# A two-layer hybrid mixer on one core: three steps of the recurrent stage start later in the program, their readers of transferred data are held in program order, and two half modulation vectors move to TensorE

## The chip, the core and the metric

The program runs on one NeuronCore of one Trainium2 chip. The metric is device time in microseconds (us) of one execution. The engines are TensorE (PE, with its weight loads PEld), VectorE (DVE), ScalarE (ACT), GpSimd (POOL) and SyncE (SP), which here issues all the transfers (DMAs). Each engine takes its instructions in one fixed order; an instruction that waits holds everything behind it on that engine.

## The reference, cut to what matters

Two layers over 1024 latent tokens and 256 context tokens of width 1024:

```python
for l in range(DEPTH):
    sh1, sc1, gt1, sh2, sc2, gt2 = split(silu(c) @ w_mod[l] + b_mod[l], 6)   # modulation; the same for c_ctx
    ux = _modulate(h, norm1_g[l], sh1, sc1) @ w_in[l]          # 17 column blocks of 128
    uc = ...                                                   # the same weights on the context
    y_rwkv = _rwkv_mixer(ux, uc, ...)                          # both directions, context state first
    h = h + gt1 * (concat([y_rwkv, pool(ux), fourier(ux), conv(ux)]) @ w_out[l])
    h = h + gt2 * _swiglu(_modulate(h, norm2_g[l], sh2, sc2), ffn_w_in[l], ffn_w_out[l])
    # the context stream hc likewise, in the first layer only
return _rmsnorm(h, final_norm_g)

# _rwkv_mixer, per head and token, in each direction:
S_t = S_{t-1} diag(w_t) + (S_{t-1} (-kk_t)) (a_t * kk_t)^T + v_t k_t^T ;  y_t = S_t r_t
```

## The kernel before

Activations stand with channels on the 128 partitions. A float32 matmul is kept exact enough by splitting each operand in a high and a low half (`split`, L317: ACT copies the high half, DVE or POOL takes the difference) and three products.

**A layer.** `rwkv1` makes the projections that the recurrence needs, while a side generator (convolution and pooling) and, in the first layer, the generators of six half modulation vectors (`s.mods`: j = 2, 3, 4 in two halves) are stepped between them. A half vector is made either by `mod_sum` (L240: for each of 8 slices of the weights, the slice times a scalar, added up, for two right-hand sides: on DVE where half is 1, on ACT and POOL where it is 0) or by `mod_pe` (8 matmuls of 512 columns with a 2-column stationary operand, a copy, 4 small matmuls). `MODPE` names those made by `mod_pe`.

**The recurrent stages** (`rwkv2`). The recurrence is done in blocks of 128 tokens, two directions at a time: 2 stages over the context and 8 over the latent, in each layer; 20 in all. Stage j goes through these steps, in different rounds `it` of the loop, each round having 14 gaps (`GAPS`):

- `prep`: decays and scaled keys (a scan on DVE, L917, and products on DVE and POOL).
- `inner`: products of keys (PE), masked by DVE into the tiles W (L982, four per stage); eight small DMAs write them to DRAM (Ad, L986), two of 256 KB bring them back spread over the partitions (As, L992). Then the solve: a triangular inverse by 8 rounds of small DVE instructions (L1020 to L1041; a small part on POOL, behind a memset of the tile, L1018). Its result goes by one DMA to DRAM (Td, L1045) and by four back into TT (L1051).
- `front_b`: the joining of the two half blocks of the inverse. DVE transposes TT (L1091), PE and ACT do two small steps (L1103, L1120); W gets a copy of the keys by DMA (L1109).
- `chain`: the recurrence itself, a row of PE steps and ACT copies, with products on POOL (L1147).
- `finish`: the read-out; DMAs bring back the other direction's part (L1196), DVE adds it (L1207).

Between the steps `W.step()` moves every live generator on by one `yield`, and `W.fill` hands PE a fixed amount of other work: first the remaining projections and the Fourier mixing, later the output projection of the blocks that are ready (`outp`, L1638). A generator that yields `None` gives up the filling of that gap.

The code sets an order only loosely: the framework rearranges the instructions of each engine by a priority list against its own estimate of when inputs are ready. `s.ahead(SPRI)` puts the solve's instructions ahead. `keep_in_program_order` ties an instruction behind the one that was written before it on the same engine.

Of the kernel before, what the change touches and what calls it, by code (L numbers as in the profile page):

```python
# [11 lines left out]
ALU = mybir.AluOpType  # L12
# [4 lines left out]
D = 1024  # L17
# [11 lines left out]
GAPS = 14  # L29
MLAG = 3  # L30
# [8 lines left out]
OLAG = 4  # L39
SIDEP = 2  # L40
MODP = 2
MODPE = ((3, 0),)
# [48 lines left out]
class _Kernel:  # L91
# [61 lines left out]
    @contextmanager  # L153
    def ahead(s, by):

        s.tc.cur_priority -= by
        yield
        s.tc.cur_priority += by

# [157 lines left out]
    def split(s, src, hi, lo, eng=None):  # L317
        s.nc.scalar.copy(hi, src)  # L318
        (eng or s.lo_eng).tensor_tensor(lo, src, hi.bitcast(F32), ALU.subtract)  # L319

# [472 lines left out]
    def rwkv2(s, R, fill):  # L793

        hss = [("c", i) for i in range(2)] + [("x", i) for i in range(8)]
        N = len(hss)
# [4 lines left out]
        for it in range(-3, N):  # L801
# [9 lines left out]
            for g in range(GAPS):  # L811
                if g == 0:
                    if 0 <= it + 1 < N:
                        if it == -1:
                            s.states(R, F[0])
                            for h in range(2):
                                s.nc.gpsimd.memset(F[0].VS[h][64 * h:64 * h + 64, :], 0.0)
                        tb_ = W.start(s.front_b(R, F[it + 1]))
                    if it >= 1 and F[it - 1].rd:
                        W.start(s.finish(R, F[it - 1]))  # L820
                if g == GAPS // 2 and 0 <= it + 2 < N:
                    F[it + 2].v = s.slices(R, "v", F[it + 2], "v")
# [14 lines left out]
            for t in (tb_ if 0 <= it + 1 < N else None, tx.get(it + 2), tp if it + 3 < N else None):  # L837
                W.drain(t)
# [125 lines left out]
    def inner(s, R, F):  # L964
# [30 lines left out]
        for d in range(2):  # L995
# [8 lines left out]
            yield  # L1004
        s.lab(f"rsolve.{F.seg}{F.i}")
# [8 lines left out]
        for a in range(2):  # L1014
# [3 lines left out]
            nc.gpsimd.memset(at(x, 16 * a, [33, 16]), 1.0)  # L1018
            with s.ahead(SPRI):
                e.tensor_tensor(t(0, [1, 2]), D(34, [33, 2]), D(1, [33, 2]), ALU.mult)  # L1020
# [37 lines left out]
    def front_b(s, R, F):  # L1058
# [4 lines left out]
        for p in range(2):  # L1063
            nc.scalar.copy(vr[:, p * 128:(p + 1) * 128], s.nat(F.v, p, 1))
# [26 lines left out]
        nc.vector.transpose(T1.rearrange("q (u i) -> q u i", i=32), TTv[:, :, 0:32])  # L1091
# [89 lines left out]
    def finish(s, R, F):  # L1181
# [20 lines left out]
        yield  # L1202
        yield
        lab()
        for t_, w_ in ((y, w[0]), (ks, w[1])):
            hv = lambda a: a.rearrange("q (d n) -> q d n", d=2)
            nc.vector.tensor_tensor(hv(t_), hv(t_), hv(w_)[:, ::-1, :], ALU.add)  # L1207
# [429 lines left out]
    def outp(s, l, tb, hi_, ho, ymix):  # L1637
# [5 lines left out]
        acts = []  # L1643
        for k in ks:
# [7 lines left out]
            s.split(y, *a)  # L1652
            acts.append(a)
            yield 0.1
# [222 lines left out]
```

## Time and profile before

| | |
|---|---|
| median of 3 runs | 3368.19 us (3366.14 to 3374.23) |
| the profiled execution | 3355.82 us; its span 3354.0 us |
| busy share of the span | PE 88%, PEld 71%, DVE 64%, POOL 42%, ACT 38% |
| mean granted TensorE clock | 0.912 of full speed |
| recurrent stages, first layer | about 462 to 924 us of the span |
| recurrent stages, second layer | about 2182 to 2610 us |

Times in the views are from the start of the span. A view of waits says which engine sat idle, at which line, until what. In the table by stretch the columns are busy time of each engine with the number of instructions, the granted clock (1.00 is 2.4 GHz), the busy share of the 16 DMA engines and GB/s.

### The profile page before, as it was taken

What the parts mean: (1) busy time and instruction counts of PE and PEld (TensorE: products, weight loads), DVE (VectorE), ACT (ScalarE), POOL (GpSimd) and SP (SyncE); (2) the same over time, 40 slices, a digit from 0 to 9 for tenths busy, and PEclk for the clock granted to TensorE, in tenths of its full rate; (3) what the DMA queues carried; (4) which work ended last, traced back from release to release, by engine and by line L of the source; (5) the groups of instructions that cost most, each with busy time, mean ns of one, the idle gap of its engine ahead of it and who ended that gap; (6) DMA issues with size and microseconds to landing.
All of it is one profiled execution on the core that took longest, in us unless ns stands there. A gap on an engine that the chain in (4) does not pass through costs nothing.

```text
span 3354.0 us, 52362 instructions
## 1 busy us (share of the span) xinstructions
PE 2962.7 (88%) x18872; PEld 2391.2 (71%) x18872; DVE 2136.8 (64%) x3524; ACT 1261.7 (38%) x2575; POOL 1395.4 (42%) x1490
## 2 busy tenths in 40 slices
PE   6978898777989999999999978878776699999998
PEld 3757766665778888887888766645554478888887
DVE  6799766666566888644535597666575655555435
ACT  4555435344463322223212455333433433333312
POOL 2465324554268544444310154245541265454600
PEclk8979887788899999999999988878877799999999
DMA  7433345555464444336412222345553322224512
GB/s 265 148 99 105 102 117 143 148 152 156 142 215 153 143 134 151 112 106 225 141 29 90 75 69 95 106 130 142 163 143 83 129 76 82 88 76 134 171 40 77
DMA packets 375818, 415.48 MB, mean 124 GB/s; under 512 B 115587, under 2 KB 214916, under 8 KB 375558
## 3 DMA queue, kind: packets, MB, share of 16 engines
q1 hardware_dynamic: 375558, 412.13, 39.5%
q8 instruction: 149, 2.44, 0.3%
q14 instruction: 111, 0.91, 0.1%
HBM read 306.49 MB, written 100.27 MB: 121 GB/s over the span
## 4 chain that ended last, share of the span: by engine, by line
PE 58%; DVE 21%; DMA 11%; issue 4%; SPq 2%; ACT 2%; POOL 1%; DVEq 0%; POOLq 0%; ACTq 0%
PE pc L151 17%; PE ps L151 17%; PE pb L151 14%; PE pf L151 10%; DVE c L525 4%; DMA t<-Ad 3%; DMA Td<-t 2%; DVE t L1039 2%; DVE t L1032 1%; DVE t L255 1%; DVE t L947 1%; DVE g L1040 1%; DVE t L1041 1%; DVE f L319 1%; DMA Ad<-t 1%
## 5 line engine op out<-in xcount | busy, mean ns | idle before, releaser
L151 PE MATMUL pc<-t,f 128*128 128x512 f32 (+1 forms) x3108 | 744.8, 389 | 31.4 <-ACT t L420 18.7
L151 PEld LDWEIGHTS pc<-t,f 128*128 128x128 f32 x3108 | 575.3, 193 | 160.3 <-ACT t L420 22.9
L151 PE MATMUL ps<-t,f 128*128 128x512 f32 (+1 forms) x2094 | 517.7, 392 | 21.3 <-ACT t L318 7.6
L151 PE MATMUL pb<-t,f 128*128 128x512 f32 (+1 forms) x2094 | 467.5, 368 | 7.8 <-ACT t L1457 3.6
L151 PEld LDWEIGHTS ps<-t,f 128*128 128x128 f32 x2094 | 390.6, 190 | 102.2 <-ACT t L318 8.1
L151 PEld LDWEIGHTS pb<-t,f 128*128 128x128 f32 x2094 | 368.7, 189 | 77.7 <-ACT t L1457 4.4
L1504 ACT CAST f<-c 128x512 fp32r<-128x512 f32 x316 | 195.8, 621 | 529.3 <-PE ps L151 127.7
L1506 POOL TENSOR_TENSOR f<-c,f 128x512 fp32r<-128x512 f32 x135 | 185.8, 1377 | 429.3 <-ACT f L1504 424.2
L151 PE MATMUL pf<-t,f 128*128 128x512 f32 (+2 forms) x1500 | 311.1, 361 | 20.9 <-DMA f<-eo 10.0
L151 PEld LDWEIGHTS pf<-t,f 128*128 128x128 f32 (+1 forms) x1500 | 247.5, 197 | 66.5 <-issue 10.4
L318 ACT CAST f<-m 128x512 fp32r<-128x512 f32 (+1 forms) x236 | 135.5, 577 | 413.4 <-PE pb L151 218.6
L1506 DVE TENSOR_TENSOR f<-c,f 128x512 fp32r<-128x512 f32 x181 | 161.8, 894 | 139.5 <-ACT f L1504 134.5
L523 POOL TENSOR_TENSOR c<-c,cp 128x352 f32<-128x352 f32 (+2 forms) x168 | 185.4, 1104 | 151.5 <-ACT c L516 91.8
L151 PE MATMUL pf<-c,f 128*128 128x512 f32 (+1 forms) x704 | 212.0, 431 | 8.5 <-DVE t L1669 7.2
L319 POOL TENSOR_TENSOR t<-c,t 128x512 fp32r<-128x512 f32 (+1 forms) x110 | 138.1, 1294 | 163.0 <-PE ps L151 100.2
L151 PE MATMUL ps<-t,t 64*128 64x128 f32 (+2 forms) x1032 | 156.1, 342 | 54.9 <-DVE t L947 32.4
L151 PEld LDWEIGHTS ps<-t,t 64*128 64x128 f32 (+1 forms) x1032 | 129.9, 230 | 82.8 <-issue 26.3
L525 DVE SCALAR_TENSOR_TENSOR c<-c,dv,c 128x352 f32<-128x352 f32 (+2 forms) x238 | 186.9, 819 | 1.0
L255 DVE SCALAR_TENSOR_TENSOR cp<-m,sc,cp 128x512 f32<-128x512 f32 x140 | 138.5, 1010 | 51.9 <-DMA m<-in_wmod 51.1
L151 PE MATMUL pc<-t,t 128*64 128x64 f32 (+3 forms) x2484 | 137.8, 246 | 33.8 <-ACT t L1165 19.7
L151 PEld LDWEIGHTS pc<-t,t 128*64 128x64 f32 (+2 forms) x2484 | 111.9, 151 | 76.8 <-issue 24.4
L151 PEld LDWEIGHTS pf<-c,f 128*128 128x128 f32 x704 | 137.4, 222 | 39.8 <-DVE t L1669 7.8
(256 smaller groups left out, 4760.6 us busy)
## 6 DMA issues: line engine op xcount, KB each, us to landing
c<-in_ffin SPq DMA_DIRECT2D x176, 256.0 KB
m<-in_wmod SPq DMA_DIRECT2D x116, 256.0 KB
t<-rw SPq DMA_DIRECT2D x232, 128.0 KB
hid<-t SPq DMA_DIRECT2D x88, 256.0 KB
c<-hid SPq DMA_DIRECT2D x88, 256.0 KB
m<-in_ffout SPq DMA_DIRECT2D x80, 256.0 KB
t<-in_wmod SPq DMA_DIRECT2D x76, 256.0 KB
m<-in_win SPq DMA_DIRECT2D x64, 256.0 KB
```

The lines of the kernel that those rows point to most:

```text
L151: s.nc.tensor.matmul(o, l, r, start=start, stop=stop)
L255: nc.vector.scalar_tensor_tensor(acc[t], w, sc, acc[t], ALU.mult, ALU.add)
L318: s.nc.scalar.copy(hi, src)
L319: (eng or s.lo_eng).tensor_tensor(lo, src, hi.bitcast(F32), ALU.subtract)
L523: nc.gpsimd.tensor_tensor(g, g, t_, ALU.add)
L525: nc.vector.scalar_tensor_tensor(a, w[:, j:j + m], tap(j), a, ALU.mult, ALU.add)
L947: nc.vector.tensor_tensor(BKv[rows, :, :, 1 - h, :], cv(kd)[rows], cv(iP)[rows], ALU.mult)
L1032: nc.vector.tensor_tensor(tv, at(x, o, [0, m], [1, 4], [32, 4]), at(T_, r0, [32, m], [0, 4], [1, 4]), ALU.mult)
L1039: nc.vector.tensor_tensor(tv, at(x, o + 4, [0, m], [1, n], [32, 4]), at(T_, r0, [32, m], [0, n], [1, 4]), ALU.mult)
L1040: nc.vector.tensor_reduce(uv, tv, mybir.AxisListType.X, ALU.add)
L1504: nc.scalar.copy(hi, x)
L1506: (nc.gpsimd if s.nw % 7 in LOP else nc.vector).tensor_tensor(lo, x, hi.bitcast(F32), ALU.subtract)
```

## The change

```diff
-MLAG = 3
+MLAG = 6
+SLAG = 2
+FLAG = 4
-MODPE = ((3, 0),)
+MODPE = ((2, 1), (3, 0), (4, 1))
+    def pin(s, i):
+        return s.tc.keep_in_program_order(i)
...
     def split(s, src, hi, lo, eng=None):
-        s.nc.scalar.copy(hi, src)
+        r = s.nc.scalar.copy(hi, src)
         (eng or s.lo_eng).tensor_tensor(lo, src, hi.bitcast(F32), ALU.subtract)
+        return r
...
+                if g == GAPS // 2:
+                    W.drain(tx.get(it + 1))
...
-            for t in (tb_ if 0 <= it + 1 < N else None, tx.get(it + 2), tp if it + 3 < N else None):
+            for t in (tb_ if 0 <= it + 1 < N else None, tp if it + 3 < N else None):
                 W.drain(t)
...
+        for _ in range(SLAG):
+            yield
         s.lab(f"rsolve.{F.seg}{F.i}")
...
-            nc.gpsimd.memset(at(x, 16 * a, [33, 16]), 1.0)
+            s.pin(nc.gpsimd.memset(at(x, 16 * a, [33, 16]), 1.0))
             with s.ahead(SPRI):
-                e.tensor_tensor(t(0, [1, 2]), D(34, [33, 2]), D(1, [33, 2]), ALU.mult)
+                s.pin(e.tensor_tensor(t(0, [1, 2]), D(34, [33, 2]), D(1, [33, 2]), ALU.mult))
...
-            nc.scalar.copy(vr[:, p * 128:(p + 1) * 128], s.nat(F.v, p, 1))
+            s.pin(nc.scalar.copy(vr[:, p * 128:(p + 1) * 128], s.nat(F.v, p, 1)))
...
-        nc.vector.transpose(T1.rearrange("q (u i) -> q u i", i=32), TTv[:, :, 0:32])
+        s.pin(nc.vector.transpose(T1.rearrange("q (u i) -> q u i", i=32), TTv[:, :, 0:32]))
...
-        yield
-        yield
+        for _ in range(FLAG):
+            yield
         lab()
...
-            nc.vector.tensor_tensor(hv(t_), hv(t_), hv(w_)[:, ::-1, :], ALU.add)
+            s.pin(nc.vector.tensor_tensor(hv(t_), hv(t_), hv(w_)[:, ::-1, :], ALU.add))
...
-            s.split(y, *a)
+            late.append((y, a))
             acts.append(a)
+        for _ in range(OLAG):
+            yield None
+        for y, a in late:
+            s.pin(s.split(y, *a))
             yield 0.1
```

The joining waits six yields instead of three, the solve two more, the read-out four instead of two; a solve may now run on into the next round and is completed at its middle gap. In `outp` the loads of a block are all issued, four gaps without filling follow, then the splits.

On DVE, around the start of the sixth solve of the first layer (its working tile is g_1091 before, g_1086 and g_1147 of two solves after), the order before was: the last reduction of the solve before, two of the four masks of this stage, the transpose of the TT that has just been sent off, two additions of the output projection, the new solve.

```order
L1033 TENSOR_REDUCE t2_744_3437<-t2_744_3437 128x8x4
L982 TENSOR_TENSOR t2_892_4342<-ps_1068_5700,cv_73 128x512
L982 TENSOR_TENSOR t2_894_4344<-ps_1069_5701,cv_73 128x512
L1091 STREAM_TRANSPOSE t2_925_4533<-t2_881_4303 128x256
L1669 SCALAR_TENSOR_TENSOR t2_1056_5600<-pf_1057_5602,mod0_78,t2_1056_5600 128x256
L1669 SCALAR_TENSOR_TENSOR t2_1076_5736<-pf_1077_5738,mod0_78,t2_1076_5736 128x256
L1020 TENSOR_TENSOR g_1091_5863<-t2_721_3310 128x4x2
```

On DVE after the change, at the start of the seventh solve of that layer, the last mask (L991) stands before the end of the solve before:

```order
L991 TENSOR_TENSOR t2_703_3190<-ps_1121_6147,cv_73 128x512
L1052 TENSOR_TENSOR t2_855_4076<-t2_855_4076,g_1086_5810 128x6x8
L1043 TENSOR_TENSOR t2_855_4076<-t2_722_3289,t2_855_4076 128x112
L1044 TENSOR_REDUCE t2_855_4076<-t2_855_4076 128x7x4
L1050 TENSOR_TENSOR t2_855_4076<-t2_722_3289,t2_855_4076 128x112
L1051 TENSOR_REDUCE g_1086_5810<-t2_855_4076 128x28
L1052 TENSOR_TENSOR t2_855_4076<-t2_855_4076,g_1086_5810 128x7x4
L1043 TENSOR_TENSOR t2_855_4076<-t2_722_3289,t2_855_4076 128x128
L1044 TENSOR_REDUCE t2_855_4076<-t2_855_4076 128x8x4
L1684 SCALAR_TENSOR_TENSOR t2_1131_6222<-pf_1132_6224,mod0_78,t2_1131_6222 128x256
L1684 SCALAR_TENSOR_TENSOR t2_1141_6282<-pf_1142_6284,mod0_78,t2_1141_6282 128x256
L1031 TENSOR_TENSOR g_1147_6347<-t2_721_3288 128x4x2
```

The transpose has moved out of this place. On DVE after the change it stands inside the seventh solve, 15 instructions behind its start:

```order
L1044 TENSOR_REDUCE t2_749_3454<-t2_749_3454 128x2x4
L1050 TENSOR_TENSOR t2_749_3454<-t2_721_3288,t2_749_3454 128x192
L1051 TENSOR_REDUCE g_1147_6347<-t2_749_3454 128x48
L1052 TENSOR_TENSOR t2_749_3454<-t2_749_3454,g_1147_6347 128x2x24
L1102 STREAM_TRANSPOSE t2_865_4144<-t2_980_4871 128x256
L926 SCALAR_TENSOR_TENSOR t2_682_3063<-t2_592_2604,t2_663_2960 128x512
```

Over the 20 stages the rows between the last mask and the solve's first instruction on DVE were 70 and are 123; the rows between the end of a solve and the transpose of its result were 2 to 7 in 16 stages and are 16 to 36 in 18. On SP, at the same place before, the four reads of TT (L1051) stood between the writes of Ad and its reads (L992):

```order
L1045 DMA Td1059_5634<-t2_744_3437 4x256x32
L986 DMA Ad1064_5668<-t2_892_4342 32x4x32 x2
L1661 DMA t2_1088_5828<-hd223_865 128x256
L1051 DMA t2_881_4303<-Td1059_5634 32x8x32 x4
L867 DMA t2_746_3469<-rw255_897 128x2x128
L1661 DMA t2_1098_5915<-hd224_866 128x256
L986 DMA Ad1064_5668<-t2_894_4344 32x4x32 x2
L1670 DMA ho213_855<-t2_1056_5600 128x256
L296 DMA m2_1108_6034<-in_wout 128x512
L992 DMA t2_721_3310<-Ad1064_5668 128x1x512
L992 DMA t2_722_3311<-Ad1064_5668 128x1x512
```

On SP after the change, for the same stage:

```order
L995 DMA Ad1055_5593<-t2_889_4308 32x4x32 x2
L995 DMA Ad1055_5593<-t2_891_4310 32x4x32 x2
L995 DMA Ad1055_5593<-t2_890_4309 32x4x32 x2
L995 DMA Ad1055_5593<-t2_892_4311 32x4x32 x2
L1056 DMA Td1062_5664<-t2_749_3454 4x256x32
L1676 DMA t2_1072_5724<-hd221_863 128x256
L1001 DMA t2_721_3288<-Ad1055_5593 128x1x512
L1001 DMA t2_722_3289<-Ad1055_5593 128x1x512
L1062 DMA t2_904_4380<-Td1062_5664 32x8x32 x4
```

The reads of TT have gone behind the reads of Ad here. Over the 20 stages they stood ahead of them in 10 and do so in 8.

## Rows read from the trace of the kernel before

**Rows 1.** The page: busy time by engine, and the chain that ended last.
```profile
PE 2962.7 (88%) x18872; PEld 2391.2 (71%) x18872; DVE 2136.8 (64%) x3524; ACT 1261.7 (38%) x2575; POOL 1395.4 (42%) x1490
...
PE 58%; DVE 21%; DMA 11%; issue 4%; SPq 2%; ACT 2%; POOL 1%; DVEq 0%; POOLq 0%; ACTq 0%
```
**Rows 2.** Stretches: first layer's modulations, the filling after, both layers' recurrent stages.
```profile
160.00:360.00 200.00, 157.45 (x784) 124.52 (x784) 197.03 (x294) 110.87 (x214) 115.26 (x113) 0.84 0.31 99
360.00:462.00 102.00, 98.51 (x589) 80.51 (x587) 64.64 (x152) 36.91 (x85) 26.05 (x55) 0.98 0.44 127
462.00:924.00 462.00, 376.78 (x3825) 289.35 (x3826) 295.58 (x641) 193.78 (x498) 218.81 (x342) 0.81 0.51 144
2182.00:2610.00 428.00, 315.23 (x3319) 231.47 (x3317) 261.19 (x586) 161.29 (x427) 180.60 (x307) 0.78 0.46 129
```
**Rows 3.** Six solve-to-solve stretches of the first layer (588 to 870), summed.
```profile
sum 282.00, PE 221.21 PEld 176.74 DVE 183.21 ACT 114.76 POOL 150.27; mean PE 36.87 PEld 29.46 DVE 30.54 ACT 19.13 POOL 25.04
```
**Rows 4.** Line L992 (reads of Ad): who waited for it, us and times.
```profile
  POOL t L1018: 206.6, 20
  DVE g L1020: 143.6, 20
```
**Rows 5.** Line L1091 (transpose of TT): what it waited for, then who waited for it.
```profile
  DMA t<-Td: 68.0, 15
...
  PE pb L151: 23.8, 3
```
**Rows 6.** DVE, from the end of one solve to the next (start, length, engine, line).
```profile
620.24 0.29 DVE L1033 TENSOR_REDUCE t<-t 128x32 f32<-128x128 f32 x1
...
623.49 0.69 DVE L982 TENSOR_TENSOR t<-ps,cv 128x512 f32<-128x512 f32 x1 [2.37 <-PE ps L151]
628.29 0.45 DVE L1091 STREAM_TRANSPOSE t<-t 128x256 f32<-128x256 f32 x1 [4.11 <-DMA t<-Td]
628.66 0.83 DVE L1669 SCALAR_TENSOR_TENSOR t<-pf,mod,t 128x256 f32<-128x256 f32 x2
636.63 0.17 DVE L1020 TENSOR_TENSOR g<-t 128x8 f32<-128x8 f32 x1 [7.14 <-DMA t<-Ad]
```
**Rows 7.** SP in the same time.
```profile
625.43 1.79 SPq L1051 DMA_DIRECT2D t<-Td  x4
...
628.55 0.86 SPq L986 DMA_DIRECT2D Ad<-t  x2
...
630.88 1.15 SPq L992 DMA_DIRECT2D t<-Ad  x2
```
**Rows 8.** DVE, a solve with no read of TT between.
```profile
2440.90 1.28 DVE L982 TENSOR_TENSOR t<-ps,cv 128x512 f32<-128x512 f32 x2
2450.80 0.17 DVE L1020 TENSOR_TENSOR g<-t 128x8 f32<-128x8 f32 x1 [5.77 <-DMA t<-Ad]
```
**Rows 9.** DVE, transposes outside such a gap, first and last of five.
```profile
676.14 0.45 DVE L1091 STREAM_TRANSPOSE t<-t 128x256 f32<-128x256 f32 x1 [6.64 <-DMA t<-Td]
...
2578.96 0.45 DVE L1091 STREAM_TRANSPOSE t<-t 128x256 f32<-128x256 f32 x1 [4.12 <-DMA t<-Td]
```
**Rows 10.** The chain of waits from 500 us: two reads of Ad.
```profile
504.57 6.26 DMA t<-Ad
...
547.97 9.23 DMA t<-Ad
```
**Rows 11.** DVE, 100 to 310 us: busy time of line L255 (count).
```profile
100.00:310.00 210.00, 40.25 (x42) 0.88 0.39 124
```
**Rows 12.** PE, one matmul of a half vector.
```profile
155.70 1.02 PE L151 MATMUL pf<-t,sc 128*2 128x512 f32 x2
```
**Rows 13.** Line L1646 (loads of the output projection): who waited.
```profile
  ACT c L318: 38.8, 11
```
**Rows 14.** Line L1669 (the output projection's addition): all of them.
```profile
L1669 DVE SCALAR_TENSOR_TENSOR t<-pf,mod,t x40: 443/740/753, 628.7 to 2495.1; 128x512 f32<-128x512 f32 x32, 128x256 f32<-128x256 f32 x8
```

More of the change, by code (lines that the diff above doesn't have):

```diff
@@ L1642, in outp @@
         s.lab("outp")
-        acts = []
+        acts, late = [], []
         for k in ks:
```

## Prediction

> **What bounds the kernel now.** I read the page first: PE is busy for 88% of the span, and the chain that ended last is 58% PE, 21% DVE and 11% DMA [rows 1]. So most of the span is bound by PE and this change does not touch it; what can be won lies where PE stands still. The table by stretch shows where: between 160 and 360 us DVE is busy for 197.0 of 200 us and PE for 157.5, so DVE sets the pace; the 102 us behind it are PE's again (98.5). In the recurrent stages PE is busy for 376.8 of 462 us in the first layer and 315.2 of 428 us in the second, at a mean granted clock of 0.81 and 0.78, and DVE for about two thirds: neither is full, so waits set the pace there [rows 2]. The reader is to see that about 198 us of PE's time stand idle in the two stretches of stages, and 42 us in the first one.
>
> The waits come next. DVE's first instruction of a solve waited 143.6 us in 20 solves for the reads of Ad, POOL's memset 206.6 us [rows 4]; the transpose of TT waited 68.0 us in 15 of 20 [rows 5]. One stage shows how they stand: the solve ends at 620.53, the last mask at 624.18, the transpose waits 4.11 us for Td until 628.29, the next solve 7.14 us for Ad until 636.63 [rows 6]. DVE thus did 2.7 us of work in 16.1 us. SP explains part of it: the four reads of TT stand ahead of the last writes of Ad, and these are issued only at 628.55, 4.4 us after the last mask; the reads of Ad follow at 630.88 [rows 7]. Where no read of TT stands between, 8.6 us passed from the last mask to the solve [rows 8], against 12.4 us here.
>
> **The stages, part by part.** The sum is made against the profiled execution, 3355.8 us, which is 12.4 us below the median of 3368.2; I add these at the end.
>
> *Delays, pins and the moved draining* go together, since what they do is one new order. Three things follow on DVE.
> - Order on SP: in ten stages the reads of TT stood ahead of the reads of Ad, now in eight. Two stages at 12.4 - 8.6 = 3.8 us: 8 us.
> - The transpose: it now stands 15 or more rows inside a solve, after its TT has long landed, so its 68.0 us go. But most of that wait lay between the last mask and the solve, where DVE would have waited for Ad anyway, as in rows 6. Only five waits lay elsewhere, 2.6 to 6.6 us each, 23.4 us in all [rows 9]. I count 23.
> - The solve: between the last mask and its start 123 rows stand now, 70 before. A row takes 295.58/641 to 261.19/586 us, 0.45 us [rows 2], so 53 rows cover 24 us of the wait for Ad.
>
> Together DVE is held 55 us less. The bounds: at most 143.6 + 68.0 = 212 us, if every one of these waits went; below nothing if the wait only moves to another engine (rivals). The 55 us are not all the kernel's. A stage lasts 47 us (282/6) and DVE works in 30.5 and PE in 36.9 of them [rows 3]: a stage of 44 us leaves PE 7 us of slack, so PE does not close the gap, but some stages will wait for PE, ACT or POOL next. I take three quarters, 41 us, since the transpose and the solve's first instruction sit on the engine whose order decides when the next stage's products and masks come.
>
> How far the wait for Ad can fall by order: the read of 256 KB alone took 6.26 and 9.23 us in the chain [rows 10]. Either it queues behind other transfers, then an earlier place shortens it too; or it is slow in itself. The Trainium skill, "DMA: Bandwidth & Descriptors", "Rules for kernel authors", says that an outermost dimension of fewer than 16, such as a broadcast of c copies, keeps a transfer on at most c of the 16 engines; this read broadcasts 4 copies outermost. By that rule the read stays near its 6 us whatever the order, and the sum stays as above; by the other reading up to 3 us a solve, 60 us in 20, would be added to it. No row here counts the engines of one transfer. I add nothing.
>
> *The read-out's two more yields and its pin, the pinned copy of v:* DVE and ACT no longer stop for transfers that come late; the waits are single and short, and ACT and DVE have slack there. Nothing, from -10 to +10 us.
>
> *The output projection's loads.* ACT waited 38.8 us in 11 of its splits for them [rows 13]; ACT is busy for less than half of the stages [rows 2], so little of that reached PE. Against it stand four more gaps without filling for each of five blocks. `FILL` gives 0.9 us of PE's time to a gap: 3.6 us a block, three blocks in the first layer, 10.8 us of matmuls that move behind the stages, where PE is full. In the second layer the filling ended at 2495 [rows 14], with stages until 2610, so it costs nothing. Between -10 and +11 us; I take 0.
>
> **The modulation vectors.** Two `mod_sum` on DVE go: 2 x 8 slices x 2 instructions, 32, at 40.25/42 = 0.96 us [rows 11]: 31 us less for DVE, in the stretch that DVE bounds. Added on PE are 16 matmuls at 1.02 us [rows 12], 16 us; the small ones at the end replace others as small. Their weight loads (DMAs) are the same. In this stretch DVE goes from 197 to 166 us and PE from 157 to 173: it can shorten by 200 - 173 = 27 us at most, and if PE stays late for other reasons the 16 us may come on top. Bounds -27 to +16; since after it PE is the bound and DVE's convolution work is spread over the steps of the generators, I take a little under half of the gain, 12 us.
>
> **Sum:** 3355.8 - 41 - 12 = 3303 us in the profiled execution, 3315 us beside the median.
>
> **Rivals.**
> *The waits move and do not go (0.16).* Four solves of 20 still have no row between the last mask and their start, and the read of Ad takes as long as ever; what DVE no longer waits at the transpose it waits at the solve, and the 41 us shrink to nothing. For it: most of the transpose's wait did lie under Ad's. Against it: the five waits elsewhere, and 53 rows. Then only the modulations are left, in full or in part: 3356 to 3368 us; I put 3358.
> *The gap closes wholly (0.10).* The 16.1 us from one solve's end to the next, with 2.7 us of work, shrink to the 8.6 us that the read path needs at least, counted from a mask that now comes before the solve's end: 7.5 us in 17 stages, 128 us; three quarters is 96, with the modulations 108, and 3260 us. For it: the first layer's later stages all have their reads of Ad first. Against it: the second layer's order gained little.
> *PE stalls at the joining (0.14), the slower side.* The transpose comes a third of a stage later, and the joining and the chain's next step stand behind it on PE. It already stopped PE three times, 23.8 us, 7.9 us each [rows 5]. In the new order the transpose is behind the solve's own wait for Ad and some 15 rows (7 us). If PE reaches the joining before that in nine stages of 20, it stalls 9 x 7.9 = 71 us, 47 more than now, and the chain behind it as well; DVE's gain is then used up by the masks that wait for PE. With 10 us for the modulations: 3368 + 47 - 10 = 3405 us. It decides from about five such stages on (5 x 7.9 = 40 us, the gain that I count in the stages). Against it: between the joining and the chain's use of it stand matmuls of the filling.
>
> **How the numbers follow.** The forecast has 0.60; within it, with the transpose and solve terms anywhere from a third to all of what DVE loses less, and the modulations from 0 to 27 us, its own range is 3265 to 3350. The range given for 8 in 10 adds the whole closing of the gap below and the moved waits and the mildest stalls above: 3250 to 3372. A measurement of this kernel can tell 0.3%, 10 us, from no change. Faster by more than that: 0.60 + 0.10 + 0.06 (the moved waits with the modulations' gain in full) = 0.76; within: 0.10; slower: 0.14.
>
> **What would show it.** Right, step by step: the waits of the transpose for Td are below 10 us in all; those of the solve's first DVE instruction fall from 143.6 to about 110 us; line L255's successor has 32 instructions fewer before 310 us and DVE is no longer full from 160 to 360 us, while that stretch ends 10 to 25 us earlier; a solve follows the last in about 44 us instead of 47. Wrong: the same 47 us with waits of DVE for PE at the masks, or of PE for the transpose above 40 us; a wait for Ad that grows by what the transpose lost; PE's busy time in the stages unchanged with its idle time at other lines.

## The result and the profile after

Sixteen runs of each kernel on the same chips: before 3360.7 us (median, 3351.3 to 3376.1), after 3343.3 us (3335.2 to 3351.5). The ratio is **0.9941, 95% interval 0.9930 to 0.9953**: 20 us faster. The forecast was 53 us. The sign was right and the time lies in the range, but the range reached from no gain at all to the whole closing of the gap, so that says little for the mechanism. The size was not right, and the question is where 33 us stayed.

The profile's page of the changed kernel: busy times by engine, and the chain that ended last (compare [rows 1]). The profiled execution took 3351.4 us, 8 us over its median.

```profile
PE 3000.7 (90%) x18888; PEld 2410.5 (72%) x18888; DVE 2109.8 (63%) x3498; ACT 1257.5 (38%) x2575; POOL 1385.8 (41%) x1484
...
PE 55%; DVE 14%; DMA 9%; issue 3%; SPq 1%; ACT 1%; POOL 1%; DVEq 0%; POOLq 0%; ACTq 0%
```

These shares can't be set beside those before: they add up to 84% here and to 99% there, because this chain could be followed back only to 514 us of the span. Its first rows are:

```profile
514.17 0.14 DVE t L1052
514.39 0.31 DVE t L1043
```

From 550 us to the end, where both chains are whole, DVE's share is 17.5% before and 16.4% after, and DMA's 10.3% and 10.2%: the chain hardly changed. The stretches, columns as in [rows 2]; the two last end at the last read-out of each layer, which comes 12 us earlier in the first (910 for 922) and 16 us earlier in the second (2594 for 2610, though that layer's first solve starts 11 us later):

```profile
160.00:360.00 200.00, 176.01 (x857) 135.91 (x856) 176.07 (x267) 115.85 (x222) 115.52 (x118) 0.87 0.27 90
360.00:462.00 102.00, 99.20 (x593) 81.95 (x592) 61.49 (x149) 37.40 (x87) 25.19 (x50) 0.98 0.41 121
462.00:910.00 448.00, 362.50 (x3662) 276.71 (x3660) 272.98 (x626) 177.62 (x467) 199.21 (x326) 0.79 0.50 141
2190.00:2594.00 404.00, 324.82 (x3307) 241.04 (x3305) 260.27 (x587) 158.64 (x425) 179.74 (x307) 0.79 0.49 137
```

DVE is no longer full from 160 to 360 us (176 us busy, 197 before). TensorE stands idle in the first layer's stages for 85 us as before (448.0 - 362.5, before 462.0 - 376.8); in the second layer's for 79 us in place of 113. Who waited for the reads of Ad, us and times (L1001, which was L992: [rows 4]); then what the transpose waited for, and who for it (L1102, which was L1091: [rows 5]):

```profile
  POOL t L1029: 173.3, 33
  DVE g L1031: 125.5, 17
```

```profile
  DMA t<-Td: 8.3, 5
...
  PE pb L153: 5.6, 5
```

So the waits went the way that was forecast: the transpose's for Td from 68.0 to 8.3 us, DVE's for Ad from 143.6 to 125.5 (about 110 was forecast), and PE waits less for the transpose than before (5.6 us for 23.8). By these waits the change does most of what it should; by the time it does a good third.

**One table for all that follows.** From each kernel's profile, by DVE's first instruction of a solve and the end of the last instruction of a read-out: A, start to first solve; B+C, from there to the second layer's first solve (B: to the first layer's last read-out); D, from there to the last read-out; E, the rest. "Pace" is the mean time between solves from the fifth to the tenth of a layer. These are single profiles. Where two kernels hold the same instructions up to the end of D (the changed one and the one with hidden halves on DVE), B differed by 8.5 us and D by 5.6, so a difference of that size in the table can be chance.

| kernel | A | B | B+C | D | E | pace, 1st / 2nd layer | ratio to before (95%) |
|---|---|---|---|---|---|---|---|
| before | 389.8 | 533.0 | 1725.8 | 495.4 | 743.1 | 47.4 / 44.8 | 1 |
| stages alone | 390.3 | 534.0 | 1732.6 | 485.4 | 751.1 | 48.0 / 44.6 | 0.9988 (0.9975 to 1.0000) |
| projection alone | 389.7 | 525.1 | 1743.6 | 487.7 | 742.8 | 46.2 / 43.6 | 1.0002 (0.9989 to 1.0016) |
| modulations alone | 386.4 | 526.4 | 1724.7 | 490.2 | 741.9 | 45.7 / 46.0 | 0.9957 (0.9941 to 0.9974) |
| all but projection | 387.7 | 533.5 | 1731.5 | 484.7 | 744.2 | 47.9 / 44.2 | 0.9967 (0.9952 to 0.9981) |
| all but modulations | 391.3 | 518.6 | 1737.4 | 474.7 | 745.0 | 44.5 / 43.0 | 0.9962 (0.9950 to 0.9974) |
| after | 389.2 | 521.3 | 1737.5 | 468.0 | 754.9 | 45.4 / 42.6 | 0.9941 (0.9930 to 0.9953) |
| before, fast reads | 388.4 | 505.2 | 1698.2 | 456.1 | 743.6 | 42.2 / 41.4 | 0.9799 (0.9785 to 0.9813) |
| after, fast reads | 384.3 | 485.9 | 1700.8 | 456.2 | 741.1 | 40.6 / 39.5 | 0.9795 (0.9773 to 0.9818) |
| best | 387.2 | 504.0 | 1697.6 | 439.1 | 742.1 | 45.2 / 38.3 | 0.9720 (0.9692 to 0.9747) |

### The profile page after: what moved, and what is told of

Same layout as the page of the kernel before. It is cut to its first block, busy times and chain, and to the rows that moved or that the text cites. A ratio compares the mean times of both kernels' runs of the same rounds, so it can differ in the third digit from the quotient of the medians.

```text
span 3349.6 us, 52386 instructions
## 1 busy us (share of the span) xinstructions
PE 3000.7 (90%) x18888; PEld 2410.5 (72%) x18888; DVE 2109.8 (63%) x3498; ACT 1257.5 (38%) x2575; POOL 1385.8 (41%) x1484
## 4 chain that ended last, share of the span: by engine, by line
PE 55%; DVE 14%; DMA 9%; issue 3%; SPq 1%; ACT 1%; POOL 1%; DVEq 0%; POOLq 0%; ACTq 0%
PE pc L153 17%; PE ps L153 17%; PE pb L153 14%; PE pf L153 8%; DMA t<-Ad 3%; DVE c L532 2%; DMA Td<-t 1%; DVE t L1050 1%; DVE t L947 1%; DVE t L1043 1%; DVE f L325 1%; DVE t L956 1%; DVE t L1469 1%; DMA t<-ho 1%; DVE t L1493 1%
## 5 line engine op out<-in xcount | busy, mean ns | idle before, releaser
L153 PE MATMUL pc<-t,f 128*128 128x512 f32 (+1 forms) x3108 | 754.4, 392 | 41.3 <-ACT t L427 16.0
L153 PE MATMUL pf<-c,f 128*128 128x512 f32 (+1 forms) x704 | 200.5, 416 | 30.0 <-DVE t L1684 20.3
L153 PEld LDWEIGHTS pc<-t,t 128*64 128x64 f32 (+2 forms) x2484 | 124.6, 161 | 71.8 <-issue 28.6
L153 PE MATMUL pc<-t,t 128*64 128x64 f32 (+3 forms) x2484 | 156.2, 258 | 20.9 <-DMA t<-t 11.8
```

Source lines behind the costliest of these rows:

```text
L153: s.nc.tensor.matmul(o, l, r, start=start, stop=stop)
```

## The parts, one by one

The first four runs leave parts out or make one alone. out_undo is the changed kernel with this edit, mod_undo with the next one, stage_only with both; out_only is the kernel before with the first edit the other way round.

```diff
-            late.append((y, a))
+            s.split(y, *a)
             acts.append(a)
-        for _ in range(OLAG):
-            yield None
-        for y, a in late:
-            s.pin(s.split(y, *a))
             yield 0.1
```

```diff
-MODPE = ((2, 1), (3, 0), (4, 1))
+MODPE = ((3, 0),)
```

> Only the delays, the pinned readers of the stages and the moved draining; output projection and modulation vectors as before. Theory (the stages gain about 40 us, the output projection's new gaps give some 20 us back, the modulations do nothing): ratio to the kernel before 0.988 to 0.990, some 37 us less; the matmuls of the filling between 600 and 922 us number about 548 again, against 480 in the changed kernel. Rival A (the 20 us lost behind the first layer's stages come from the later read-out of the context, which holds the filling back): ratio 0.994, 480 matmuls. Rival B (the two modulation vectors on TensorE cost what is lost): 0.989 as well, but the next run then parts it from the theory.

> The changed kernel with the two half modulation vectors on DVE again. Theory: ratio to before 0.993 to 0.995, the same as the changed kernel within 3 us, with DVE busy about 197 us again between 160 and 360 us. Rival B (they cost 16 us of TensorE that nothing pays back): 0.989. Forecast's own term (they win 12 us): 0.998.

> The changed kernel with the output projection's splits directly behind their loads and without the four gaps that give up their filling. Theory: 0.988 to 0.990, 15 to 20 us faster than the changed kernel, with about 548 matmuls of the filling between 600 and 922 us and the waits of ACT for the loads back at some 39 us. Rival A (later read-out of the context): 0.994, as the changed kernel.

> The kernel before with the output projection's change alone. Theory: 10 to 20 us slower than before, ratio 1.003 to 1.006, since the matmuls that the new gaps give up run behind the first layer's stages, where TensorE is full. Rival A: no change, 0.999 to 1.001. The forecast's term was 0 with bounds of -10 and +11 us.

Measured: 0.9988, 0.9962, 0.9967, 1.0002. My theory failed in all four. I had read section B in the two profiles (12 us shorter) as the stages' gain, and the 12 us more in B+C as the price of the projection's given-up gaps. But without the projection's change B is 533.5 and 534.0 us, as before: in the first layer the stages had gained nothing, and B is shorter where 107 matmuls of the filling have gone out of it (587 to 480). The stretches 600 to 922 and 922 to 1080 us, instructions that write or read tile pf alone, all but projection and then after (columns PE, PEld, DVE, ACT, clock, DMA):

```profile
600.00:922.00 322.00, 136.28 (x587) 100.96 (x588) 16.58 (x26) 0.77 (x2) 0.85 0.56 159
922.00:1080.00 158.00, 76.47 (x567) 74.33 (x565) 5.00 (x12) 4.54 (x12) 0.95 0.53 174
```

```profile
600.00:922.00 322.00, 117.92 (x480) 85.43 (x480) 15.58 (x24) 0.00 (x0) 0.81 0.53 152
922.00:1080.00 158.00, 90.49 (x672) 87.25 (x672) 5.85 (x14) 5.29 (x14) 0.96 0.55 181
```

The stages alone are worth 4 us (0 to 8); with the projection, that is without the modulations, 13 us (9 to 17). The modulations and the projection without the stages were not run. And yet DVE waits in the kernel with the stages alone 105.5 us for Ad (143.6 before) and 2.7 us for Td (68.0). Where these 103 us went shows in DVE's waits from 600 to 830 us, before and with the stages alone (us, times, longest):

```profile
DVE g L1020 <- DMA t<-Ad: 29.5, 5, 7.1
DVE t L1091 <- DMA t<-Td: 21.4, 5, 6.6
DVE t L982 <- PE ps L151: 5.3, 4, 2.4
DVE t L1669 <- PE pf L151: 5.2, 2, 2.7
```

```profile
DVE t L1680 <- PE pf L153: 27.4, 7, 6.9
DVE g L1031 <- DMA t<-Ad: 11.1, 2, 8.8
DVE t L1680 <- DMA t<-hd: 9.1, 1, 9.1
DVE t L926 <- POOL t L921: 8.0, 4, 4.8
DVE t L956 <- ACT t L928: 4.8, 1, 4.8
```

50.9 us of waits for Ad and Td became 11.1; in their place DVE waits for the filling's product (L1680 was L1669: 27.4 us for 5.2), its loads, POOL and ACT. Over the whole of section B (389.8 to 922.8 us before, 390.3 to 924.3 with the stages alone) it is the same:

```profile
DVE g L1020 <- DMA t<-Ad: 62.2, 10, 9.7
DVE t L1091 <- DMA t<-Td: 29.0, 7, 6.6
DVE t L1669 <- PE pf L151: 8.9, 4, 2.7
DVE t L347 <- ACT t L346: 4.8, 3, 2.1
```

```profile
DVE g L1031 <- DMA t<-Ad: 43.0, 6, 11.4
DVE t L1102 <- DMA t<-Td: 2.5, 2, 1.5
DVE t L1680 <- PE pf L153: 35.5, 9, 6.9
DVE t L354 <- ACT t L353: 29.3, 6, 15.5
```

The waits for Ad and Td are 45.7 us less; those for the filling's product and for the reciprocal of a norm (L354, which was L347) are 51.1 us more. In all, DVE sits idle in section B for 195 us before and for 202 us with the stages alone. The longest of the new waits in full, with the stages alone: first ACT, then DVE, then POOL.

```profile
828.00 1.75 ACT L339 ACTIVATE t<-t 128x256 f32<-128x256 f32 x5 [9.30 <-DMA t<-ho]
```

```profile
832.64 0.95 DVE L354 RECIPROCAL t<-t 128x128 f32<-128x128 f32 x1 [15.53 <-ACT t L353]
833.51 0.10 DVE L1031 TENSOR_TENSOR g<-t 128x8 f32<-128x8 f32 x1
```

```profile
821.68 0.13 POOL L1029 MEMSET t<- 128x16 f32 x1 [6.28 <-DMA t<-Ad]
```

ACT stops 9.3 us at a norm's load, DVE 15.5 us at a reciprocal that needs ACT, and the solve stands behind it, though its first read of Ad had landed 12 us before (POOL's memset, which waits for the same read, runs at 821.7). The instruction that waits is another; a stage takes 48.0 us as it took 47.4. This one stop, just ahead of the tenth solve, is also in the other kernels that have the stages' change but not the projection's in the first layer (15.2 to 18.2 us; 5.7 with the additional filling of fat_undo), and not where the projection's change is there too (1.3 to 4.1 us with the reads as they were). Even so it is not what the time hangs on: nogap, below, has 4.1 us of it, and its section B is as long (532.6 us) as that of the kernel with all but the projection (533.5), which has 16.3.

**Gaps or late splits? One layer or both?** nogap, then l2only, against the changed kernel:

```diff
             acts.append(a)
-        for _ in range(OLAG):
-            yield None
         for y, a in late:
```

```diff
-            late.append((y, a))
             acts.append(a)
-        for _ in range(OLAG):
+            if l == 0:
+                s.split(y, *a)
+                yield 0.1
+            else:
+                late.append((y, a))
+        for _ in range(OLAG * l):
             yield None
```

> The changed kernel without the four gaps that the output projection gives up ahead of its splits; the splits still stand behind all the loads and are tied to program order. The first runs gave 0.9988 for the stages alone, 1.0002 for the projection alone and 0.9941 for all. Theory now (the pace of a stage is set by TensorE with its filling; the given-up gaps take filling out of the stages, so that these get shorter, the first layer pays it back behind its stages, the second does not): without the gaps as the changed kernel without the projection's part, 0.996 to 0.997; second layer's first solve at about 2120 us (changed kernel 2126.7), from it to the last read-out about 484 us (changed kernel 467). Rival A (what helps is that ACT no longer stops at the splits, not the gaps): 0.993 to 0.995 with 467 to 472 us there.

> The changed kernel with the output projection's change in the second layer alone; in the first its splits stand directly behind their loads, without the gaps. Theory: first layer as without it (second layer's first solve at about 2120 us, 7 us before the changed kernel's), second layer as the changed kernel (467 to 475 us from there to the last read-out): ratio to before 0.992, some 6 us faster than the changed kernel. Rival (the gaps in the first layer cost nothing in all, and the sections differ by chance): 0.994 to 0.996.

nogap: 0.9970 (0.9959 to 0.9982), first solve at 2117.1 us, D 489.1: as expected, so it is the gaps that help, not the late splits. They help in the second layer (D 468.0 for 489.1), where the filling ends at 2504 us for 2480. That it helps there because it then lies in the last stages, where PE is least busy, is argued and was not tried by itself. l2only: 0.9935 (0.9923 to 0.9948), 3340.6 us; its first layer came out as expected (first solve 2120.9), D with 477.8 longer. It is 2 us faster than the changed kernel and not 6, within what can't be told.

**The modulation vectors alone**, the second edit above the other way round in the kernel before.

> The kernel before with the two half modulation vectors on TensorE alone. Two pairs so far say 7 us (0.9962 to 0.9941, 0.9988 to 0.9967), each with some 5 us of uncertainty; the profiles show 0 to 3 us at the first solve. Theory (they win 7 us): 0.9975 to 0.9985. Rival (nothing, what the first solve shows): 0.9995 to 1.0005. The forecast's own term: 0.9965.

0.9957 (0.9941 to 0.9974): 14 us (9 to 20), more than the theory's 5 to 8 us; the forecast's own 12 us fits. The two pairs in the table, 0.9962 to 0.9941 and 0.9988 to 0.9967, give 7 us each with some 6 of uncertainty. So the vectors carry 7 to 14 us, a third or more of the whole. After the result I had put them at nothing, since the first solve stands where it stood; in this profile it is 3.4 us earlier, and the rest shows in no one section.

## What sets the pace of a stage

**TensorE?** More filling in the first layer's stages (fat_undo, on out_undo), and less: one product in place of three in the output projection's filling (lean_before, lean_undo).

```diff
-FILL = ((2.6, 1.2, 0.9), (2.3, 1.0, 0.9))
+FILL = ((2.6, 1.2, 1.2), (2.3, 1.0, 0.9))
```

```diff
-                s.mm(ps[:, :n], wh, ah, i == 0, False)
-                s.mm(ps[:, :n], wh, al, False, False)
-                s.mm(ps[:, :n], wl, ah, False, i == len(acts) - 1)
+                s.mm(ps[:, :n], wh, ah, i == 0, i == len(acts) - 1)
```

> The changed kernel with the output projection as before and more filling in each gap of the first layer's stages, 1.2 us for 0.9, 4.2 us of TensorE's time more a stage. Without that the first layer's stages follow each other in 47.9 us (fifth to tenth solve). If TensorE sets the pace there: 51 to 53 us, and the time as without it (0.9967) within 5 us, since what is filled earlier is not to do later. If the loop through the read of Ad sets it: 47 to 49 us, some 25 to 35 us of filling come for nothing, the second layer's first solve stands at about 2090 us (2119 without it), ratio 0.987 to 0.990.

> The kernel before with one of the three products of the output projection's filling (it leaves out the two products with a low half, so its filling takes a third of TensorE's time; the gaps, the copies and the transfers stay). It is read by the pace of the stages, from the fifth to the tenth solve of a layer: 47.4 and 44.7 us in the kernel before. If TensorE's work sets that pace: some 8 us less, 39 to 41 us in the first layer. If DVE's waits for Td and Ad set it: 45 to 47 us.

> The same cut in the changed kernel with the output projection as before (47.9 and 43 us a stage with the whole filling). If the forecast's 41 us for the stages are there but covered by TensorE's work: 3 us a stage or more below the kernel before with the same cut. If the shorter waits of DVE are worth nothing in themselves, since the read of Ad still stands in the loop: within 1 us of it.

More filling: 0.9971 (0.9956 to 0.9986) for 0.9967; the pace is 48.5 for 47.9, which is what the read's theory asked, but the time is what TensorE's theory asked. The pace misleads here, since the 16.3 us stop of the section above lies in the 47.9 and only 5.7 us of it in the 48.5. By section B, which is 28.6 us longer while the stretch from there to the second layer is 29.2 shorter, a stage is 2.9 us longer for 4.2 us more filling.

Less filling (one execution of each): 45.5 us a stage before and 48.8 in the changed kernel without its projection's part (second layer 41.5 and 42.4), where TensorE's theory asked for 39 to 41. The 3 us a stage by which the changed kernel is behind in the first layer are that same stop again:

```profile
833.10 0.95 DVE L354 RECIPROCAL t<-t 128x128 f32<-128x128 f32 x1 [18.18 <-ACT t L353]
```

It is 1.8 us in the kernel before with the cut, and this makes 16.4 of the 16.5 us by which the five steps from solve to solve differ (244.2 for 227.7 us). So TensorE's work counts, 2 to 3 us a stage either way, but does not set the pace by itself, and no gain of 3 us a stage lies hidden under it. One thing blunts this test, 589 to 826 us before with the whole filling and with the cut:

```profile
589.00:826.00 237.00, 183.70 (x1922) 148.21 (x1923) 155.71 (x326) 97.92 (x250) 134.37 (x204) 0.80 0.56 153
589.00:826.00 237.00, 173.30 (x1823) 135.23 (x1821) 162.17 (x345) 104.44 (x272) 143.62 (x220) 0.70 0.60 169
```

The mean granted clock is 0.70 of 2.4 GHz with the cut, 0.80 without it. The filling's own products (tile pf) fell from 91.6 to 53.3 us of TensorE's time there, all its work only from 183.7 to 173.3: the work that was cut came back in part as slower work.

**The read of Ad?** as16, then as2, against the changed kernel:

```diff
-            nc.sync.dma_start(As[a], Adf[:, a * 512:(a + 1) * 512].unsqueeze(0).broadcast_to([4, 32, 512]))
+            for c in range(4):
+                nc.sync.dma_start(As[a][32 * c:32 * c + 32, :], Adf[:, a * 512:(a + 1) * 512])
```

```diff
-            nc.sync.dma_start(As[a], Adf[:, a * 512:(a + 1) * 512].unsqueeze(0).broadcast_to([4, 32, 512]))
+            for c in range(2):
+                nc.sync.dma_start(As[a][64 * c:64 * c + 64, :], Adf[:, a * 512:(a + 1) * 512].unsqueeze(0).broadcast_to([2, 32, 512]))
```

> The changed kernel with each of the two reads of Ad split in four DMAs of 32 partitions, one for each copy, in place of one DMA with a broadcast of four outermost. Theory on its size (the Trainium skill, page DMA: Bandwidth & Descriptors, section Rules for kernel authors: an outermost dimension of 4 keeps a transfer on 4 engines): a read lands 2 to 4 us after its issue, against 6 to 9, and the waits for Ad at the solve fall from 125 us to under 60 us. By the pace theory (TensorE sets the pace of a stage) the time gains 0 to 5 us at most: 0.9925 to 0.994. Rival A (the solve's wait for Ad still sets the pace): 20 solves times 3 us, 0.980 of before at best, some 45 us. Rival B (the read queues behind other transfers, and six more issues on SP make every later transfer late): 0.996 or above.

> The changed kernel with each of the two reads of Ad in two DMAs of 64 partitions with a broadcast of two outermost. It parts two reasons for the gain of the four-way split. By the rule of the Trainium skill (DMA: Bandwidth & Descriptors, Rules for kernel authors) each of them is kept to 2 engines, 64 KB for each engine as in the one DMA with a broadcast of four: the read stays at 6 to 9 us and the ratio at 0.993 to 0.995. If it is the number of DMAs that run side by side, about half of the gain: 0.986 to 0.988.

The same bytes in four DMAs of 32 partitions: 0.9795 (0.9773 to 0.9818), **some 50 us faster** than the changed kernel (49 by the ratios, 53 by the medians); the waits for Ad fell from 125.5 to 68.8 us. In two DMAs with a broadcast of two: 1.0212 (1.0199 to 1.0226), 90 us slower. (The text expected waits under 60 us. Of its times, that of the rival by which the wait for Ad sets the pace came nearest, with 0.980 at best.) So the number of DMAs by itself is not it, since two were worse than one; the four differ from both in their shape, 32 partitions outermost and no broadcast. Reads of Ad and writes of Td in the chain of waits (start, length), first after, then as2, then as16 with the write of Td split as well:

```profile
628.76 8.47 DMA t<-Ad
669.99 10.09 DMA t<-Ad
2476.11 5.10 DMA Td<-t
```

```profile
732.95 8.10 DMA t<-Ad
2319.55 11.85 DMA t<-Ad
```

```profile
2266.18 1.95 DMA Td<-t
2270.48 1.81 DMA t<-Ad
```

The Trainium skill's rule (DMA: Bandwidth & Descriptors, Rules for kernel authors) is that an outermost dimension below 16 keeps a transfer to at most so many engines. The traces agree: in the chains of waits a read took 5.8 to 11.1 us in the changed kernel and 1.6 to 3.4 us in pieces, a write of Td 5.1 us or more and 2.0 in pieces. The write has no broadcast, so it is not the broadcast alone. I had taken from the rule that as2 would change nothing, 64 KB for each engine as before. Measured, the kernel is 90 us slower; why two smaller DMAs are worse than one stays open, since no row counts the engines of a transfer.

The pace tells the same: with the fast reads a stage of the first layer takes 42.2 us for 47.4 before the change and 40.6 for 45.4 after it. The read of Ad is in the loop of a stage in both kernels, with some 5 us.

**What is the change worth without the slow reads?** as16_before and as2_before are the same edits in the kernel before; the two with td16 also write Td in pieces:

```diff
-        nc.sync.dma_start(Td.rearrange("b u h (m par) i -> par (b u h) m i", par=4), Tt[:, 0:256])
+        for c in range(4):
+            nc.sync.dma_start(Td.rearrange("b u h (m par) i -> par (b u h) m i", par=4)[c], Tt[32 * c:32 * c + 32, 0:256])
```

> The kernel before with the reads of Ad split in four DMAs of 32 partitions, and nothing of the change. In the changed kernel this split was worth 54 us (0.9941 to 0.9795). Theory (the way from the masks through the write and the read of Ad to the solve sets the pace of a stage in both kernels, and the change only moved which instruction waits): about the same 54 us, ratio to before 0.983 to 0.986. Rival (in the kernel before the waits of the transpose for Td hold DVE in any case, and a shorter read is lost in them): 20 us or less, 0.994 or above.

> The changed kernel with the reads of Ad split as before, and the write of Td, whose outermost dimension is 4 too, split in four DMAs of 32 partitions. In the chain of waits one write of Td took 4.8 us in the kernel before. Theory (the round trip of Td is off the pace in the changed kernel, whose transposes wait for it only 8 us in all): 0 to 8 us on top of the split reads, ratio 0.977 to 0.980. Rival (the round trip of Td is in the loop as that of Ad is): about 2 us a solve, 40 us, 0.967 to 0.969.

> The kernel before with both short transfers (reads of Ad and write of Td in pieces of 32 partitions) and nothing of the change. With the reads alone the two kernels were equal, 0.9799 and 0.9795; with both the changed one has 0.9752. Theory (all that the change gains is the hiding of transfers that are slow by their shape): 0.974 to 0.977. Rival (the new order is worth some 20 us by itself once Td is short as well): 0.980 or above.

> The kernel before with each read of Ad in two DMAs with a broadcast of two outermost, which made the changed kernel 90 us slower (1.0212). With fast reads the two kernels are equal (0.9799 and 0.9795), with the reads as they were the changed one is 20 us ahead. Theory (all that the change gains is the hiding of part of the slow reads): with slower reads it is ahead by more than 20 us, this kernel 1.030 to 1.040. Rival (its gain has nothing to do with the length of the reads): 1.027, 20 us as before.

| reads of Ad | before | after | lead of after |
|---|---|---|---|
| slower still (as2) | 1.0248 (1.0228 to 1.0268) | 1.0212 (1.0199 to 1.0226) | 12 us |
| as they were | 1 | 0.9941 (0.9930 to 0.9953) | 20 us |
| fast (as16) | 0.9799 (0.9785 to 0.9813) | 0.9795 (0.9773 to 0.9818) | 1 us |
| fast, and write of Td | 0.9766 (0.9741 to 0.9792) | 0.9752 (0.9737 to 0.9768) | 5 us |

Each lead is uncertain by 8 to 10 us, the 20 us by 4. With fast reads the lead is gone within that, and D is equal (456.1 and 456.2). as16_before gained 67 us, more than the 54 that its theory asked (0.983 to 0.986). The dose does not go on: with slower reads the lead is 12 us and not more than 20 (as2_before missed its 1.030), so "all that the change gains is the hiding of slow reads" is more than these runs show. What they show is that the reads were worth 67 us by themselves and that the change is hardly worth anything beside them. The split write of Td gave 14 us on top (expected 0 to 8, or 40), and 11 us in the kernel before.

**The version that beats both.** hid_dve has this edit in the changed kernel; best has it with the td16 and l2only edits.

```diff
-                        s.split(x, *hr[f - f0][tb], nc.gpsimd)
+                        s.split(x, *hr[f - f0][tb], nc.vector if last else nc.gpsimd)
```

> The changed kernel with the low halves of the hidden activations in the second layer's last products made by DVE in place of POOL (44 instructions of 0.7 us). In the profile of the changed kernel one such DVE instruction of 0.67 us took 11.2 us beside 12 instructions of POOL without a gap (14.9 us), and TensorE stood still for 7.2 us; from the last read-out to the end it took 741 us, the kernel before 730. Theory (POOL holds DVE off, and TensorE waits for it): no DVE instruction of that line over 2 us, 729 to 733 us for that section, ratio 0.991 to 0.9925. Rival A (the held instruction is an accident of the one profiled run): 0.994. Rival B (DVE becomes late with the halves itself, 30 us more work): 0.996 or above.

> The changed kernel with all that helped or did no harm: both short transfers, the output projection's change in the second layer alone, and the low halves of the hidden activations on DVE in the second layer. If their gains add (2 us each beside the transfers, both within what was uncertain): 0.973 to 0.975. If they don't: 0.9752 as with the transfers alone, or above it if the shorter stages make DVE late in the last products.

hid_dve: 0.9936 (0.9924 to 0.9948), the same as the changed kernel; E is 744.3 us, for 754.9 in the one profile of the changed kernel. (The 741 and 730 us in its text are counted from a later instruction than E.) See the last section. best: **0.9720 (0.9692 to 0.9747), 3267.8 us** (expected 0.973 to 0.975), 75 us ahead of the changed kernel. Some 64 us of it are the transfers' shape, as as16_td16 shows; the 11 us of the two other edits are at the edge of what can be told.

## Why the prediction was right or wrong

- *"Together DVE is held 55 us less ... I take three quarters, 41 us, since the transpose and the solve's first instruction sit on the engine whose order decides"*: **this step failed**. The premise held (the waits fell by 59.7 and 18.1 us), the conclusion did not: 41 us were forecast and the stages gave 4 us (0 to 8) alone, 13 us (9 to 17) together with the projection. That a wait shorter at one instruction of DVE is time saved for the stage was taken over at three quarters without a row that showed it. What the runs show in its place is the first rival, "the waits move and do not go", to which I gave 0.16; but it had the place wrong. The wait does not pass to the solve's Ad, it passes to what stands next in DVE's order, the filling's product and a norm that needs ACT (45.7 us less and 51.1 us more in section B). Its 3358 us were too slow as well, since the projection's gaps add a gain. In the second layer some 10 us of D came, and 6 to 7 us of them went again in B+C, as far as single profiles can tell.
- *"How far the wait for Ad can fall by order ... I add nothing"*: right as far as order goes, since the read stayed at 6 to 11 us in the changed kernel. But the passage held the larger thing: the rule named what was wrong with the read, and I used it only to say that order would not help. A better shape gave some 50 us (67 on the kernel before). That the 60 us which I set aside are near this is luck: they stood for a read that queues behind others.
- *The output projection, 0, from -10 to +11*: alone 1.0002, so right; but with the stages' change its gaps give some 10 us (0.9970 to 0.9941). I had said that it "costs nothing" in the second layer; it gains there.
- *The modulations, -12*: right in size (7 to 14 us), and with the gaps it is most of why the sign came out right; that "that stretch ends 10 to 25 us earlier" was wrong (first solve 389.8 to 389.2). Where the gain appears stays open, so the mechanism of this term is not shown.
- *The stall at the joining*, the slower side: PE waited 5.6 us for the transpose; not seen. *The whole closing of the gap*: not seen either, with a pace of 45.4 and 42.6 us.
- *The read-out's yields and the pinned copy of v, 0*: not tried by themselves.
- *The readings*: DVE's work in [rows 6] is 2.5 us of the 16.1 (16.1 less the three waits), not 2.7; no term hangs on it.
- Of the signs that I named, the transpose (below 10 us: 8.3), the fewer instructions of `mod_sum` (28 of the 32 are on that line: 42 to 14) and DVE from 160 to 360 us came; the solve's wait (about 110: 125.5) and the pace of 44 us (45.4 and 42.6) came in part. A sign of being wrong came in part in the first layer: TensorE's idle time stayed at 85 us there. The signs of being right could not tell a wait that goes from one that moves; the parts alone could.

## What to carry to other kernels

A wait that an engine no longer has is not time that the program no longer takes: ask what the same engine stops at next, and leave parts out before believing a sum over two profiles, whose sections can differ by some 8 us by themselves. A mean over five stages can hang on one stop: look at the single steps before calling it a pace. Where a transfer stands in the chain again and again, look at its shape before its place: four pieces with 32 partitions outermost did in one edit more than twice what the whole change did. And work that is moved out of a stretch makes the stretch shorter without any gain; count instructions of the filling in it before calling it faster.

## What the hardware did that I had not expected

In two of the twenty profiles (after, and the stages alone) one DVE instruction that takes 0.68 us elsewhere took 11 us. After, first DVE, then POOL:

```profile
3100.18 11.20 DVE L325 TENSOR_TENSOR f<-m,f 128x512 fp32r<-128x512 f32 x1 [3.54 <-ACT f L324]
...
3111.96 0.68 DVE L325 TENSOR_TENSOR f<-m,f 128x512 fp32r<-128x512 f32 x1
```

```profile
3095.93 14.89 POOL L325 TENSOR_TENSOR t<-c,t 128x512 fp32r<-128x512 f32 x12
```

POOL runs 23 instructions without a gap from 3081.63 to 3110.82 (the row has those from 3096 us on); DVE's ends 0.56 us behind the last of them. TensorE stood still for 7.2 us until it ended and had a mean granted clock of 0.74 from 3100 to 3120 us. Section E shows the price: 754.9 and 751.1 us in these two profiles, 741 to 745 in all others. That fits the 8 us by which the profiled execution lay above its median.

The Trainium skill (SBUF — State Buffer, section SBUF: two separate sides) says that a DVE instruction with two inputs in SBUF and a POOL instruction that reads SBUF lock each other out for a whole instruction. The same profile agrees: of 33 such DVE instructions (this line, 128x512) that came up while one of POOL's ran, 26 ended 0.55 us behind the end of POOL's, after 0.7 to 1.8 us; of 120 with none beside them, none took over 0.70 us. The one above is more than that: it was held through eight more of POOL's that started behind its own start. Why it lost eight times in a row, in these two profiles alone, is not shown.

With the same halves made by DVE none is over 2 us and E is 744.3; but so it is in the 17 other profiles without that stop, and the time is the same (0.9936 for 0.9941). So the rival of that run, that the stop is an accident of single executions, is not ruled out.
